# Second layer of a hybrid decoder: an earlier block transpose, other gaps in the scan, and moved turnings

## The chip, the cores and the metric

The kernel runs on one core of a Trainium2 chip. The metric is the device time of one execution in microseconds (us). The profile's engines are PE (TensorE), DVE (VectorE), ACT (ScalarE), POOL (GpSimd) and SP (SyncE), each of which takes its instructions in program order.

## The reference

Two residual layers over 512 positions of width 2048 in float32. The first is gated differential attention, which the change does not touch. The second is RWKV-7 time mixing with 32 heads of 64 channels: after one input projection and a token shift, each head keeps a 64 x 64 state S that is updated at each position, and its output is normalised, gated and projected.

```python
def step(S, inp):
    r_t, w_t, k_t, v_t, a_t, b_t = inp
    sa = jnp.einsum('bhvk,bhk->bhv', S, a_t)
    S = S * w_t[:, :, None, :] + sa[..., None] * b_t[:, :, None, :] + v_t[..., None] * k_t[:, :, None, :]
    y = jnp.einsum('bhvk,bhk->bhv', S, r_t)
    return S, y
...
kk = kk / jnp.maximum(jnp.sqrt(jnp.sum(kk * kk, axis=-1, keepdims=True)), 1e-12)
k = k * (1.0 + (a - 1.0) * k_a.astype(F32))
y = wkv7_scan(rh, heads(decay), kh, vh, -kk, kk * ah)
...
x = x + (y * silu(g)) @ w_out
```

## The kernel before

The second layer goes through 16 rounds j, each for a pair of heads (128 channels). A round is paced by projections on PE: v, then k of the next pair, the gate of an earlier pair (from j = 3, LAG), and r of the next pair. One projection is 16 slices of the 2048 inputs times three products, hH and hL being the two parts of the activations and wh and wl those of the weights: 48 matmuls pp (L129) of 128 x 512. ACT makes each wh (L115), DVE each wl (L116).

The recurrence is done in 8 chunks of 64 positions. For each pair, `gram` multiplies keys with keys and queries into gp. ACT copies parts of gp to LP and all of it to G. DVE turns LP into LT (a stream transpose, L1214), and `t_solve` solves a unit triangular system in 31 steps of two DVE instructions (tmpl, L1227, and Tm, L1230), with n the reciprocal norm. Two transposes give T (L1235) and W (L1240). `t_first` multiplies G's blocks with T into px (32 small matmuls, L1261), `t_second` finishes the blocks in TT. POOL copies W into TT (L1246) and zeroes G's upper parts (`mask_gram`, two selects for each head, L1180 and L1182).

The scan (`scan_pair`) of a pair runs one round later. For each chunk c: sm from VS and G on PE (L1353), rhs on ACT (L1356), sm from TT and rhs (L1366), VS on ACT (L1368), sm from VS and BKT (L1373), and the new state VS on DVE (L1377, or L1380 for c = 0), which the next chunk's first sm needs. `turn_keys` (L1195) and `turn_values` (L1303) turn BK and mixv by PE.

`tick` counts projection matmuls. A generator that yields n is taken up again n matmuls later: the solve by its own counts, the scan by gap, gap and gap_s (in full rounds, 3 <= j < 15, these are 7, 7 and 8). Hooks in `unit_chan` do the same at a matmul's number in a projection. `behind` ties an instruction to a matmul for the order only; the chip does not wait there. A list scheduler with priorities (scan 5000, solve 4000, urgent 2000) makes each engine's order out of this. `g.soon` and `g.later` are lists of pieces that are issued behind an ACT copy and behind a state copy of the scan.

Of the kernel before, what the change touches and what calls it, by code (L numbers as in the profile page):

```python
# [23 lines left out]
P = 128  # L24
# [928 lines left out]
C = 64  # L953
# [74 lines left out]
LAG = 3  # L1028
# [6 lines left out]
def mus(g, i, j):  # L1035
    n = i * 16 + j
    return g.mu[:, n : n + 1], g.omu[:, n : n + 1]
# [6 lines left out]
    g.nc.tensor.matmul(out, ones, l[:], start=False, stop=True)  # L1044


def soon(g):
    while g.soon:
        g.soon.pop(0)()


def stage1(g, j, k, up):
# [73 lines left out]
def gram(g, j, p):  # L1126

    nc, w, BK = g.nc, g.work, p.BK
    p.G = w.tile([P, NC_, 2, 2, C], F32, name="G1", tag="G1", bufs=2)
    halves = []  # L1130
    for c0, tag in ((0, "pb"), (4, "pc")):
        gp = [g.ps.tile([P, 512], F32, name="gp", tag=tag, bufs=2) for _ in range(2)]
        halves.append((c0, gp))
        for i in range(4):
            for h, r_ in ((0, slice(0, C)), (1, slice(C, P))):
                m = nc.tensor.matmul(gp[h][:, i * P : (i + 1) * P], BK[r_, c0 + i, :, :], p.AR[r_, c0 + i, :, :],
                                     start=True, stop=True)
    p.LP = w.tile([P, NC_, HALF], F32, name="LP", tag="tmpl", bufs=1)
    with g.tc.high_priority(offset=AHEAD):
        for c0, gp in halves:  # L1140
            for h in range(2):
                for half in range(2):
                    q, o = h * C + half * HALF, half * HALF
                    nc.scalar.copy(p.LP[q : q + HALF, c0 : c0 + 4],
                                   gp[h][q : q + HALF].rearrange("p (u x) -> p u x", u=4)[:, :, o : o + HALF])

    def grams():
        for c0, gp in halves:
            for h in range(2):
                nc.scalar.copy(p.G[:, c0 : c0 + 4, :, h, :], gp[h][:].rearrange("p (u x t) -> p u x t", u=4, x=2))  # L1150

    g.soon.append(grams)
    if not j:
        soon(g)


def norms(g, j, p, m):
# [49 lines left out]
def t_solve(g, j, p):  # L1207


    nc, w = g.nc, g.work  # L1210
    NQ = HALF // NG
    yield 9
    LT = w.tile([P, HALF, HALF], F32, name="LT", tag="LT", bufs=1)
    lt = nc.vector.transpose(LT[:].rearrange("p (r c) t -> p t r c", r=NG),  # L1214
                        p.LP[:].rearrange("p c t -> p t c")[:, :, None, :].to_broadcast([P, HALF, NG, NC_]))
    Tm = w.tile([P, NQ, HALF], F32, name="Tm", tag="Tm", bufs=1)
    tmp = w.tile([P, NQ * HALF], F32, name="tmpl", tag="tmpl", bufs=1)
    nc.gpsimd.tensor_copy(Tm[:], g.unit[:])
    n2 = p.n2
    behind(g, lt)  # L1220
    with g.tc.issue_after(lt.ins):
        nc.vector.tensor_scalar(n2[:], n2[:], 1e-24, None, ALU.max)
        nc.vector.reciprocal(n2[:], n2[:])
    for i in range(HALF - 1):
        n, s = HALF - 1 - i, i // NG + 1
        tt = tmp[:, : n * s].rearrange("p (a b) -> p a b", a=s)
        st = nc.vector.scalar_tensor_tensor(tt, LT[:, i : i + 1, i + 1 :].to_broadcast([P, s, n]), n2[:, i : i + 1],  # L1227
                                       Tm[:, 0:s, i : i + 1].to_broadcast([P, s, n]), ALU.mult, ALU.mult)
        behind(g, st)
        nc.vector.tensor_add(Tm[:, 0:s, i + 1 :], Tm[:, 0:s, i + 1 :], tt)  # L1230
        yield 3 + i % 2
    nc.vector.tensor_mul(Tm[:], Tm[:], n2[:, None, :].to_broadcast([P, NQ, HALF]))
    p.T1 = w.tile([P, NC_, HALF], F32, name="T1", tag="T1", bufs=1)
    yield 9
    tt = nc.vector.transpose(p.T1[:].rearrange("p c (q r) -> p q r c", r=NG),  # L1235
                        Tm[:].rearrange("p q (r c) -> p q r c", r=NG))
    p.W = w.tile([P, NC_, HALF], F32, name="W", tag="Tm", bufs=1)
    behind(g, tt)
    yield 4
    tt = nc.vector.transpose(p.W[:], p.T1[:])  # L1240
    behind(g, tt)
    for h in range(2):
        for half in range(2):
            o = half * HALF
            q = slice(h * C + o, h * C + o + HALF)
            nc.gpsimd.tensor_copy(g.TT[j % 2][q, :, h, o : o + HALF], p.W[q])  # L1246
# [95 lines left out]
def scan_pair(g, j, p, gap, gap_s, others):  # L1342

    nc, w, VS = g.nc, g.work, p.VS
    both = lambda ap: ap.rearrange("p h n -> p (h n)")
    p.SA = w.tile([P, NC_ - 1, C], F32, name="SA", tag="SA", bufs=1)
    for h, r_ in HEADS:
        nc.gpsimd.memset(VS[r_, 0, h, :], 0.0)  # L1350
    for c in range(NC_):
        sm = g.ps.tile([P, 512], F32, name="sm", tag="pa", bufs=1)
        nc.tensor.matmul(sm[:, 0:P], both(p.G[:, c, 0]), both(VS[:, c]), start=True, stop=True)  # L1353
        rhs = w.tile([P, C], F32, name="rhs", tag="rhs", bufs=2)
        for h, r_ in HEADS:
            rc = nc.scalar.copy(rhs[r_, :], sm[r_, h * C : h * C + C])  # L1356
        with g.tc.issue_after(rc.ins):
            soon(g)
        if c:
            for h, r_ in HEADS:  # L1360
                nc.gpsimd.tensor_copy(p.SA[r_, c - 1, :], VS[r_, c, h, :])  # L1361
        if 0 < c < NC_ - 1:
            Sg = w.tile([P, C], F32, name="Sg", tag="Sg", bufs=2)
            nc.gpsimd.tensor_scalar(Sg[:], p.SA[:, c - 1, :], p.gam[:, c : c + 1], None, ALU.mult)
        yield gap
        nc.tensor.matmul(sm[:, P : P + C], both(g.TT[j % 2][:, c]), rhs[:], start=True, stop=True)  # L1366
        for h, r_ in HEADS:
            nc.scalar.copy(VS[r_, c, h, :], sm[r_, P : P + C])  # L1368
        yield gap
        if c == NC_ - 1:  # L1370
            break
        o = P + C
        nc.tensor.matmul(sm[:, o : o + P], p.BKT[:, c, :], both(VS[:, c]), start=True, stop=True)  # L1373
        for h, r_ in HEADS:
            s_ = sm[r_, o + h * C : o + h * C + C]
            if c:
                g.state = nc.vector.scalar_tensor_tensor(VS[r_, c + 1, h, :], s_, p.gam[r_, c : c + 1], Sg[r_, :],  # L1377
                                                         ALU.mult, ALU.add)
            else:
                nc.vector.tensor_scalar(VS[r_, c + 1, h, :], s_, p.gam[r_, c : c + 1], None, ALU.mult)  # L1380
# [57 lines left out]
def layer1(g, aps):  # L1438
    nc, tc = g.nc, g.tc
    with ExitStack() as cx:  # L1440
# [5 lines left out]
        pairs = []  # L1446

        def proj(i, j, **k):
            return unit_chan(g, [(win, i * D + j * P, P)], P, **k)[0]

        def begin(j):
            c0 = j * P
            u = g.wraw.tile([RK, 2, P], F32, name="upw", tag="wraw")
            nc.sync.dma_start(out=u[:, 0, :], in_=aps["rw_decay_up"][0, :, c0 : c0 + P])
            nc.sync.dma_start(out=u[:, 1, :], in_=aps["rw_iclr_up"][0, :, c0 : c0 + P])
            up = split_act(g, u[:], w, "up")
            pairs.append(stage1(g, j, shift_mix(g, proj(1, j), P, *mus(g, 1, j), "k", 1), up))

        def receptances(j):
            def piece(f, i, p):  # L1460
# [5 lines left out]
            behind = [(39, lambda m: norms(g, j, pairs[j], m))]  # L1466
            if j:
                behind += [(6, lambda m: [mask_gram(g, pairs[j - 1], h, m) for h in range(2)]),
                           (12, piece(t_first, j - 1, pairs[j - 1])), (33, piece(t_second, j - 1, pairs[j - 1]))]
            return shift_mix(g, proj(0, j, behind=behind), P, *mus(g, 0, j), "r", 1)  # L1470

        begin(0)
# [1 line left out]
        for j in range(D // P):  # L1474
            p = pairs[j]
            if j:
# [16 lines left out]
            if j + 1 == D // P:  # L1493
                hooks.append((39, lambda m, p=p: [mask_gram(g, p, h, m) for h in range(2)]))
            stage_v(g, j, p, proj(2, j, behind=hooks))
            if j == 0:
                turn_keys(g, p, 0)
                turn_keys(g, p, 4)
                turn_values(g, p)
            if j + 1 < D // P:  # L1500
                begin(j + 1)
            if j >= LAG:
                gated(g, j - LAG, pairs[j - LAG], gate(g, j - LAG, proj(3, j - LAG)))
            if j + 1 < D // P:
                r = receptances(j + 1)
                if j:
                    with tc.high_priority(offset=AHEAD):
                        group_norm(g, j - 1, pairs[j - 1])
        chain(g, j, p, 66, 5, 6, whole=True)
        gated(g, j - 2, pairs[j - 2], gate(g, j - 2, proj(3, j - 2)))  # L1510
        gps = proj(3, j - 1)
        group_norm(g, j - 1, pairs[j - 1])
# [74 lines left out]
def body(ctx, tc, nc, aps):  # L1587
    g = Ctx()
    g.nc, g.tc = nc, tc
    g.last, g.first = None, []  # L1590
    g.chains, g.later, g.soon, g.state, g.solve = [], [], [], None, None
    g.const = ctx.enter_context(tc.tile_pool(name="const", bufs=1))
    g.hp = ctx.enter_context(tc.tile_pool(name="hp", bufs=16))
    g.wraw = ctx.enter_context(tc.tile_pool(name="wrawp", bufs=3))
# [35 lines left out]
```

## Time and profile before

| | us |
|---|---|
| median of three runs | 2161.68 (2160.67 to 2164.62) |
| the profiled execution | 2163.93 |
| its span | 2162.2 |
| PE busy | 2130.9 (99%) |
| DVE busy | 1547.3 (72%) |
| ACT busy | 1125.5 (52%) |
| POOL busy | 335.2 (16%) |

The granted TensorE clock was 0.998 of full speed. The second layer's rounds begin at about 1000 us. A full round is some 60 us long. A row of the timeline gives the start in us, the duration in us, the engine, the line, the operation and its tiles, and in brackets the idle time ahead of it and what ended it. A row of the waits gives who waited for whom, the total in us, how often, and the longest.

### The profile page before, as it was taken

To read this page: it belongs to the slowest core of one execution; us is meant where nothing else is said; L and a number is where in the kernel's file an instruction comes from. 1 tells how busy PE (TensorE), PEld (TensorE's weight loads), DVE (VectorE), ACT (ScalarE), POOL (GpSimd) and SP (SyncE) were. 2 spreads that over 40 slices of the span, in tenths; PEclk is the share of its full clock that TensorE was granted. 3 is DMA by queue.
4 is the path that set the end of the run, shared out by engine and by line. 5 is a ranking of instruction groups with operands and counts; after the bars stand their busy time and mean duration, and the time that the engine had idled before them with its cause. 6 is when DMAs were issued, how large, how long until landed. Compare 5 with 4: busy or idle time off the path is not lost.

```text
span 2162.2 us, 34954 instructions
## 1 busy us (share of the span) xinstructions
PE 2130.9 (99%) x12260; PEld 1752.8 (81%) x12260; DVE 1547.3 (72%) x4137; ACT 1125.5 (52%) x2587; POOL 335.2 (16%) x614
## 2 busy tenths in 40 slices
PE   9999999999999999999999999999999999999999
PEld 8888888888888878887777888888888888877887
DVE  5665647465656667457888988888888898887645
ACT  6443434343444455345666666666666666655333
POOL 0000000000000000011133322223333322232001
PEclk9999999999999999999999999999999999999999
DMA  6223232322223365663222233222232222345565
GB/s 196 90 86 100 79 99 87 98 89 88 97 88 97 99 198 182 185 139 87 73 69 65 67 81 85 76 77 76 78 85 77 77 68 79 89 118 186 179 169 120
DMA packets 258624, 225.77 MB, mean 104 GB/s; under 512 B 12336, under 2 KB 220480, under 8 KB 258448
## 3 DMA queue, kind: packets, MB, share of 16 engines
q1 hardware_dynamic: 239504, 188.03, 29.2%
q0 software_dynamic: 10080, 19.50, 4.5%
q10 hardware_dynamic: 8864, 16.01, 2.0%
q8 instruction: 96, 1.57, 0.3%
q14 instruction: 80, 0.66, 0.1%
HBM read 207.50 MB, written 15.99 MB: 103 GB/s over the span
## 4 chain that ended last, share of the span: by engine, by line
PE 85%; DVE 11%; issue 2%; ACT 1%; DMA 1%; POOL 0%; DVEq 0%; ACTq 0%; POOLq 0%
PE pp L129 66%; PE pt L129 5%; DVE wl L116 2%; DVE LT L1214 1%; PE sm L1353 1%; PE o L129 1%; PE sc L129 1%; PE lora L129 1%; PE sm L1373 1%; PE sm L1366 1%; DMA yr<-yd 1%; DVE tmpl L1227 1%; PE Y L1395 1%; DVE Tm L1230 1%; PE pt L346 1%
## 5 line engine op out<-in xcount | busy, mean ns | idle before, releaser
L116 DVE TENSOR_TENSOR wl<-wraw,wh 128x512 fp32r<-128x512 f32 (+1 forms) x636 | 446.9, 705 | 383.7 <-ACT wh L115 374.5
L115 ACT CAST wh<-wraw 128x512 fp32r<-128x512 f32 (+1 forms) x636 | 392.9, 619 | 516.9 <-PE pp L129 407.8
L129 PE MATMUL pp<-wh,hH 128*128 128x512 f32 x1268 | 500.3, 395 | 1.2 <-DVE prmin_rw_mu_dram L234 0.6
L129 PE MATMUL pp<-wh,hL 128*128 128x512 f32 x1268 | 497.6, 393 | 0.0
L129 PE MATMUL pp<-wl,hH 128*128 128x512 f32 x1268 | 497.1, 392 | 0.0
L129 PE MATMUL pp<-hH,wh 128*128 128x512 f32 x1024 | 417.7, 408 | 0.0
L129 PE MATMUL pp<-hH,wl 128*128 128x512 f32 x1024 | 413.3, 404 | 0.0
L129 PE MATMUL pp<-hL,wh 128*128 128x512 f32 x1024 | 413.3, 404 | 0.0
L129 PEld LDWEIGHTS pp<-wh,hH 128*128 128x128 f32 x1268 | 238.3, 188 | 50.0 <-issue 1.6
L129 PEld LDWEIGHTS pp<-wh,hL 128*128 128x128 f32 x1268 | 238.2, 188 | 48.6
L129 PEld LDWEIGHTS pp<-wl,hH 128*128 128x128 f32 x1268 | 238.4, 188 | 46.8
L129 PEld LDWEIGHTS pp<-hH,wh 128*128 128x128 f32 x1024 | 193.2, 189 | 37.8 <-issue 2.0
L129 PEld LDWEIGHTS pp<-hH,wl 128*128 128x128 f32 x1024 | 193.6, 189 | 33.4
L129 PEld LDWEIGHTS pp<-hL,wh 128*128 128x128 f32 x1024 | 193.5, 189 | 32.2
L1361 POOL COPY SA<-VS 64x64 f32<-64x64 f32 x224 | 78.0, 348 | 472.6 <-DVE VS L1377 406.9
L1227 DVE SCALAR_TENSOR_TENSOR tmpl<-LT,n,Tm 128x60 f32<-128x60 f32 (+24 forms) x496 | 136.2, 275 | 13.8
L500 POOL DMA_DIRECT2D frow<-yd x12 | 8.9, 743 | 807.6 <-DVE rs_t L67 675.8
L1230 DVE TENSOR_TENSOR Tm<-Tm,tmpl 128x60 f32<-128x60 f32 (+24 forms) x496 | 114.1, 230 | 13.2
L1356 ACT COPY rhs<-sm 64x64 f32<-64x64 f32 x256 | 52.7, 206 | 61.8 <-PE sm L1353 58.9
L1368 ACT COPY VS<-sm 64x64 f32<-64x64 f32 x256 | 53.0, 207 | 59.1 <-PE sm L1366 48.0
L1353 PEld LDWEIGHTS sm<-VS,G 128*128 128x128 f32 x256 | 45.0, 189 | 29.8 <-PE pp L129 12.9
L1377 DVE SCALAR_TENSOR_TENSOR VS<-sm,gam,Sg 64x64 f32<-64x64 f32 x192 | 54.1, 282 | 18.7 <-PE sm L1373 14.2
(339 smaller groups left out, 3261.9 us busy)
## 6 DMA issues: line engine op xcount, KB each, us to landing
wraw<-in_rw_w_in_dram SPq DMA_DIRECT2D x128, 512.0 KB, 4.0
wraw<-in_da_w_in_dram SPq DMA_DIRECT2D x254, 256.0 KB, 3.0
wraw<-in_da_w_out_dram SPq DMA_DIRECT2D x26, 512.0 KB, 4.4
wraw<-in_rw_w_out_dram SPq DMA_DIRECT2D x26, 512.0 KB, 4.1
yr<-yd SPq DMA_DIRECT2D x28, 256.0 KB, 3.4
frow<-yd POOLq DMA_DIRECT2D x12, 512.0 KB, 6.2
xq<-in_x_dram SPq DMA_DIRECT2D x16, 256.0 KB, 5.0
xd<-xq ACTq DMA_DIRECT2D x16, 256.0 KB, 3.9
```

The source lines that it names most:

```text
L115: nc.scalar.copy(hi[:], raw[:, k : k + n])
L116: nc.vector.tensor_sub(lo[:], raw[:, k : k + n], hi[:].bitcast(F32))
L129: m = nc.tensor.matmul(out, a, b, start=s, stop=e, skip_group_check=skip)
L346: nc.tensor.transpose(pt[:, c * P : (c + 1) * P], t1s[t][:, c * P : (c + 1) * P], g.ident[:])
L1214: lt = nc.vector.transpose(LT[:].rearrange("p (r c) t -> p t r c", r=NG), p.LP[:].rearrange("p c t -> p t c")[:, :, None, :].to_broadcast( ...
L1227: st = nc.vector.scalar_tensor_tensor(tt, LT[:, i : i + 1, i + 1 :].to_broadcast([P, s, n]), n2[:, i : i + 1], Tm[:, 0:s, i : i + 1].to_br ...
L1230: nc.vector.tensor_add(Tm[:, 0:s, i + 1 :], Tm[:, 0:s, i + 1 :], tt)
L1353: nc.tensor.matmul(sm[:, 0:P], both(p.G[:, c, 0]), both(VS[:, c]), start=True, stop=True)
L1356: rc = nc.scalar.copy(rhs[r_, :], sm[r_, h * C : h * C + C])
L1361: nc.gpsimd.tensor_copy(p.SA[r_, c - 1, :], VS[r_, c, h, :])
L1368: nc.scalar.copy(VS[r_, c, h, :], sm[r_, P : P + C])
L1377: g.state = nc.vector.scalar_tensor_tensor(VS[r_, c + 1, h, :], s_, p.gam[r_, c : c + 1], Sg[r_, :], ALU.mult, ALU.add)
```

## The change

Seven edits, all in the second layer. The G copies (`grams`) are split in two: the first half stays behind the rhs copies of the scan, the second half goes behind a VS copy (`g.late`). The solve's first wait goes from 9 to 5 matmuls, so that LT is asked for sooner, and a new wait of 9 (6 before j = LAG) stands between the reciprocal and the first step. In rounds 1 and 2 the steps follow each other by 2 and 3 matmuls in place of 3 and 4. `t_first` is hooked to matmul 15 of the r projection, not 12. In round 0 the turnings of keys and values move from behind the v projection into the next k projection (at 9, 15 and 27). In the last round the scan's gaps go from 4, 4 and 5 to 6, 6 and 7. The last pair's scan starts 8 matmuls into the projections that follow, not 66.

```diff
--- before.py
+++ after.py
@@ -1044,9 +1044,10 @@
     g.nc.tensor.matmul(out, ones, l[:], start=False, stop=True)
 
 
-def soon(g):
-    while g.soon:
-        g.soon.pop(0)()
+def soon(g, pieces=None):
+    pieces = g.soon if pieces is None else pieces
+    while pieces:
+        pieces.pop(0)()
 
 
 def stage1(g, j, k, up):
@@ -1144,14 +1145,15 @@
                     nc.scalar.copy(p.LP[q : q + HALF, c0 : c0 + 4],
                                    gp[h][q : q + HALF].rearrange("p (u x) -> p u x", u=4)[:, :, o : o + HALF])
 
-    def grams():
-        for c0, gp in halves:
-            for h in range(2):
-                nc.scalar.copy(p.G[:, c0 : c0 + 4, :, h, :], gp[h][:].rearrange("p (u x t) -> p u x t", u=4, x=2))
-
-    g.soon.append(grams)
+    def grams(c0, gp):
+        for h in range(2):
+            nc.scalar.copy(p.G[:, c0 : c0 + 4, :, h, :], gp[h][:].rearrange("p (u x t) -> p u x t", u=4, x=2))
+
+    g.soon.append(lambda: grams(*halves[0]))
+    g.late.append(lambda: grams(*halves[1]))
     if not j:
         soon(g)
+        soon(g, g.late)
 
 
 def norms(g, j, p, m):
@@ -1209,7 +1211,7 @@
 
     nc, w = g.nc, g.work
     NQ = HALF // NG
-    yield 9
+    yield 5
     LT = w.tile([P, HALF, HALF], F32, name="LT", tag="LT", bufs=1)
     lt = nc.vector.transpose(LT[:].rearrange("p (r c) t -> p t r c", r=NG),
                         p.LP[:].rearrange("p c t -> p t c")[:, :, None, :].to_broadcast([P, HALF, NG, NC_]))
@@ -1221,6 +1223,7 @@
     with g.tc.issue_after(lt.ins):
         nc.vector.tensor_scalar(n2[:], n2[:], 1e-24, None, ALU.max)
         nc.vector.reciprocal(n2[:], n2[:])
+    yield 9 if j >= LAG else 6
     for i in range(HALF - 1):
         n, s = HALF - 1 - i, i // NG + 1
         tt = tmp[:, : n * s].rearrange("p (a b) -> p a b", a=s)
@@ -1228,7 +1231,7 @@
                                        Tm[:, 0:s, i : i + 1].to_broadcast([P, s, n]), ALU.mult, ALU.mult)
         behind(g, st)
         nc.vector.tensor_add(Tm[:, 0:s, i + 1 :], Tm[:, 0:s, i + 1 :], tt)
-        yield 3 + i % 2
+        yield (2 if 0 < j < LAG else 3) + i % 2
     nc.vector.tensor_mul(Tm[:], Tm[:], n2[:, None, :].to_broadcast([P, NQ, HALF]))
     p.T1 = w.tile([P, NC_, HALF], F32, name="T1", tag="T1", bufs=1)
     yield 9
@@ -1365,7 +1368,9 @@
         yield gap
         nc.tensor.matmul(sm[:, P : P + C], both(g.TT[j % 2][:, c]), rhs[:], start=True, stop=True)
         for h, r_ in HEADS:
-            nc.scalar.copy(VS[r_, c, h, :], sm[r_, P : P + C])
+            vc = nc.scalar.copy(VS[r_, c, h, :], sm[r_, P : P + C])
+        with g.tc.issue_after(vc.ins):
+            soon(g, g.late)
         yield gap
         if c == NC_ - 1:
             break
@@ -1448,13 +1453,14 @@
         def proj(i, j, **k):
             return unit_chan(g, [(win, i * D + j * P, P)], P, **k)[0]
 
-        def begin(j):
+        def begin(j, turns=()):
             c0 = j * P
             u = g.wraw.tile([RK, 2, P], F32, name="upw", tag="wraw")
             nc.sync.dma_start(out=u[:, 0, :], in_=aps["rw_decay_up"][0, :, c0 : c0 + P])
             nc.sync.dma_start(out=u[:, 1, :], in_=aps["rw_iclr_up"][0, :, c0 : c0 + P])
             up = split_act(g, u[:], w, "up")
-            pairs.append(stage1(g, j, shift_mix(g, proj(1, j), P, *mus(g, 1, j), "k", 1), up))
+            pairs.append(stage1(g, j, shift_mix(g, proj(1, j, behind=turns), P, *mus(g, 1, j), "k", 1),
+                                up))
 
         def receptances(j):
             def piece(f, i, p):
@@ -1466,7 +1472,8 @@
             behind = [(39, lambda m: norms(g, j, pairs[j], m))]
             if j:
                 behind += [(6, lambda m: [mask_gram(g, pairs[j - 1], h, m) for h in range(2)]),
-                           (12, piece(t_first, j - 1, pairs[j - 1])), (33, piece(t_second, j - 1, pairs[j - 1]))]
+                           (15, piece(t_first, j - 1, pairs[j - 1])),
+                           (33, piece(t_second, j - 1, pairs[j - 1]))]
             return shift_mix(g, proj(0, j, behind=behind), P, *mus(g, 0, j), "r", 1)
 
         begin(0)
@@ -1479,7 +1486,7 @@
                 if j > 1:
                     others.append((5, lambda i=j - 2: finish_y(g, i, pairs[i])))
                 full = LAG <= j < D // P - 1
-                gaps = (7, 8) if full else (5, 6) if j == 2 else (4, 5)
+                gaps = (7, 8) if full else (5, 6) if j == 2 else (4, 5) if j == 1 else (6, 7)
                 chain(g, j - 1, pairs[j - 1], 3 if j > 1 else 22, *gaps, others)
             stage2(g, j, r, p)
 
@@ -1493,12 +1500,12 @@
             if j + 1 == D // P:
                 hooks.append((39, lambda m, p=p: [mask_gram(g, p, h, m) for h in range(2)]))
             stage_v(g, j, p, proj(2, j, behind=hooks))
+            turns = ()
             if j == 0:
-                turn_keys(g, p, 0)
-                turn_keys(g, p, 4)
-                turn_values(g, p)
+                turns = ((9, lambda m: turn_keys(g, p, 0)), (15, lambda m: turn_keys(g, p, 4)),
+                         (27, lambda m: turn_values(g, p)))
             if j + 1 < D // P:
-                begin(j + 1)
+                begin(j + 1, turns)
             if j >= LAG:
                 gated(g, j - LAG, pairs[j - LAG], gate(g, j - LAG, proj(3, j - LAG)))
             if j + 1 < D // P:
@@ -1506,7 +1513,7 @@
                 if j:
                     with tc.high_priority(offset=AHEAD):
                         group_norm(g, j - 1, pairs[j - 1])
-        chain(g, j, p, 66, 5, 6, whole=True)
+        chain(g, j, p, 8, 5, 6, whole=True)
         gated(g, j - 2, pairs[j - 2], gate(g, j - 2, proj(3, j - 2)))
         gps = proj(3, j - 1)
         group_norm(g, j - 1, pairs[j - 1])
@@ -1588,7 +1595,7 @@
     g = Ctx()
     g.nc, g.tc = nc, tc
     g.last, g.first = None, []
-    g.chains, g.later, g.soon, g.state, g.solve = [], [], [], None, None
+    g.chains, g.later, g.soon, g.late, g.state, g.solve = [], [], [], [], None, None
     g.const = ctx.enter_context(tc.tile_pool(name="const", bufs=1))
     g.hp = ctx.enter_context(tc.tile_pool(name="hp", bufs=16))
     g.wraw = ctx.enter_context(tc.tile_pool(name="wrawp", bufs=3))
```

In the order of the engines this shows at three places of a full round; round 8 (some 1480 to 1540 us) stands for all twelve. First DVE, from before LT to the state copy of chunk 1, before the change (VS is the state copy, wl the low part of a weight tile):

```order
L116 TENSOR_TENSOR wl<-wraw,wh 128x512
L1214 STREAM_TRANSPOSE LT<-LP 128x32x32
L1222 TENSOR_SCALAR n_15564<-n_15564 128x32
L1223 RECIPROCAL n_15564<-n_15564 128x32
L1227 SCALAR_TENSOR_TENSOR tmpl<-LT,n_15564,Tm 128x31
L1230 TENSOR_TENSOR Tm<-Tm,tmpl 128x31
L1227 SCALAR_TENSOR_TENSOR tmpl<-LT,n_15564,Tm 128x30
L1230 TENSOR_TENSOR Tm<-Tm,tmpl 128x30
L116 TENSOR_TENSOR wl<-wraw,wh 128x512
L1377 SCALAR_TENSOR_TENSOR VS<-sm,gam,Sg 64x64 x2
```

and after it:

```order
L1216 STREAM_TRANSPOSE LT<-LP 128x32x32
L1224 TENSOR_SCALAR n_15564<-n_15564 128x32
L116 TENSOR_TENSOR wl<-wraw,wh 128x512
L1225 RECIPROCAL n_15564<-n_15564 128x32
L1230 SCALAR_TENSOR_TENSOR tmpl<-LT,n_15564,Tm 128x31
L1233 TENSOR_TENSOR Tm<-Tm,tmpl 128x31
L1230 SCALAR_TENSOR_TENSOR tmpl<-LT,n_15564,Tm 128x30
L1233 TENSOR_TENSOR Tm<-Tm,tmpl 128x30
L1230 SCALAR_TENSOR_TENSOR tmpl<-LT,n_15564,Tm 128x29
L1233 TENSOR_TENSOR Tm<-Tm,tmpl 128x29
L116 TENSOR_TENSOR wl<-wraw,wh 128x512
L1382 SCALAR_TENSOR_TENSOR VS<-sm,gam,Sg 64x64 x2
```

The wl ahead of LT now stands behind it, and three steps instead of two stand ahead of VS.

Second PE, at the end of the scan, from the matmul that gives the state after chunk 6 to the first sm of chunk 7, before the change (pp is a projection):

```order
L1373 MATMUL sm<-VS,BKT 128x128
L129 MATMUL pp<-hH,wl 128x512
L129 MATMUL pp<-hH,wh 128x512
L129 MATMUL pp<-hL,wh 128x512
L129 MATMUL pp<-hH,wl 128x512
L129 MATMUL pp<-hH,wh 128x512
L129 MATMUL pp<-hL,wh 128x512
L129 MATMUL pp<-hH,wl 128x512
L1261 MATMUL px<-T_16073,G_15643 32x32 x16
L129 MATMUL pp<-hH,wh 128x512
L1353 MATMUL sm<-VS,G_14922 128x128
```

and after it:

```order
L129 MATMUL pp<-hH,wl 128x512
L129 MATMUL pp<-hH,wh 128x512
L129 MATMUL pp<-hL,wh 128x512
L129 MATMUL pp<-hH,wl 128x512
L129 MATMUL pp<-hH,wh 128x512
L129 MATMUL pp<-hL,wh 128x512
L129 MATMUL pp<-hH,wl 128x512
L129 MATMUL pp<-hH,wh 128x512
L1356 MATMUL sm<-VS,G_14922 128x128
L129 MATMUL pp<-hL,wh 128x512
L129 MATMUL pp<-hH,wl 128x512
L1264 MATMUL px<-T_16089,G_15643 32x32 x16
```

px now follows the sm of chunk 7; seven pp, px and one pp stood between the two sm, now eight pp.

Third POOL, beside that place, before the change (AFFINE_SELECT zeroes part of G, SA and Sg belong to the scan):

```order
L1364 TENSOR_SCALAR Sg<-SA,gam 128x64
L1180 AFFINE_SELECT G_15643<-G_15643 64x8x64
L1246 COPY TT_10024<-W 32x8x32 x4
L1361 COPY SA<-VS 64x64
L1182 AFFINE_SELECT G_15643<-G_15643 64x8x128
L1361 COPY SA<-VS 64x64
L1180 AFFINE_SELECT G_15643<-G_15643 64x8x64
L1182 AFFINE_SELECT G_15643<-G_15643 64x8x128
```

and after it:

```order
L1367 TENSOR_SCALAR Sg<-SA,gam 128x64
L1182 AFFINE_SELECT G_15643<-G_15643 64x8x64
L1184 AFFINE_SELECT G_15643<-G_15643 64x8x128
L1364 COPY SA<-VS 64x64
L1182 AFFINE_SELECT G_15643<-G_15643 64x8x64
L1364 COPY SA<-VS 64x64
L1249 COPY TT_10024<-W 32x8x32 x4
L1184 AFFINE_SELECT G_15643<-G_15643 64x8x128
```

The first large select has moved ahead of an SA copy and of the W copies into TT, right behind the first small one.

## The prediction

> **What bounds the kernel now.** I read the page's first lines, then PE's waits in the second layer, then the busy time of one round in the middle, then the timelines of DVE, PE and POOL at the places where the change puts instructions into another order. Line numbers are those of the kernel before.
>
> The page's span and engine totals (busy us, share, instructions):
>
> ```profile
> span 2162.2 us, 34954 instructions
> PE 2130.9 (99%) x12260; PEld 1752.8 (81%) x12260; DVE 1547.3 (72%) x4137; ACT 1125.5 (52%) x2587; POOL 335.2 (16%) x614
> ```
>
> PE is busy 99% of the span, so the time falls only where a wait of PE goes, and rises by every wait that is added. The view of waits for PE, from 1000 us on (engine and line, what it waited for: us in total, times, longest):
>
> ```profile
> PE sm L1353 <- DVE VS L1377: 9.3, 16, 2.2
> PE pt L1303 <- DVE Tm L1230: 3.0, 1, 3.0
> PE sm L1353 <- DVE VS L1380: 2.4, 2, 1.2
> PE px L1261 <- DVE T L1235: 1.9, 3, 0.9
> PE pt L1044 <- DVE sLx L917: 0.5, 1, 0.5
> ```
>
> These 17.1 us are all there is to gain by moving work, and nearly all of it is PE waiting for DVE. Is DVE a reserve? The window of 40 us around the solve of a full round (columns: us; PE, PEld, DVE, ACT and POOL busy with counts; clock; DMA share; GB/s):
>
> ```profile
> 1497.00:1537.00 40.00, 39.63 (x228) 32.77 (x227) 37.16 (x104) 25.23 (x61) 10.68 (x21) 1.00 0.26 69
> ```
>
> DVE is busy 37.16 of 40 us: while a solve runs it has no idle time to hide a later place in its queue. It takes instructions in program order, so what stands ahead of a state copy (VS, L1377) is paid by the next step of the scan. The twelve full rounds (j=3 to 14) run the same order, so I work out one and multiply.
>
> **The change part by part.** *The state after chunk 1, twelve times.* DVE and then PE before (start, duration):
>
> ```profile
> 1497.52 2.23 DVE L1214 STREAM_TRANSPOSE LT<-LP 128x1024 f32<-128x1024 f32 x1
> 1500.28 0.25 DVE L1227 SCALAR_TENSOR_TENSOR tmpl<-LT,n,Tm 128x31 f32<-128x31 f32 x1
> 1500.79 0.25 DVE L1227 SCALAR_TENSOR_TENSOR tmpl<-LT,n,Tm 128x30 f32<-128x30 f32 x1
> 1501.19 0.69 DVE L116 TENSOR_TENSOR wl<-wraw,wh 128x512 fp32r<-128x512 f32 x1
> 1501.91 0.60 DVE L1377 SCALAR_TENSOR_TENSOR VS<-sm,gam,Sg 64x64 f32<-64x64 f32 x2
> ...
> 1499.64 0.38 PE L1373 MATMUL sm<-VS,BKT 128*128 128x128 f32 x2
> 1501.67 0.39 PE L129 MATMUL pp<-hH,wh 128*128 128x512 f32 x1
> 1501.89 0.39 PE L129 MATMUL pp<-hL,wh 128*128 128x512 f32 x1
> 1502.65 0.46 PE L1353 MATMUL sm<-VS,G 128*128 128x128 f32 x2 [0.37 <-DVE VS L1377]
> ```
>
> The matmul that gives the state ends at 1500.02, yet the copy starts at 1501.91: it stands in DVE's queue behind two solve steps and a wl, and PE waits 0.37. In the new order LT starts one wl sooner, but the wl then stands behind it, and three steps instead of two come ahead of the copy. The same work plus one step: a step costs 0.51 (1500.28 to 1500.79). This wait is the end of the path already, so I add 0.51; bounds 0.46 (the two instructions without a gap, 0.25 and the 0.21 of a Tm, below) and 0.6 (should POOL slow one of them a little).
>
> *The state after chunk 6, twelve times.* DVE, PE and POOL there, with two rows of round 1 (1117 us) for comparison:
>
> ```profile
> 1529.44 0.21 DVE L1230 TENSOR_TENSOR Tm<-Tm,tmpl 128x16 f32<-128x16 f32 x1
> 1530.17 0.63 DVE L1227 SCALAR_TENSOR_TENSOR tmpl<-LT,n,Tm 128x8 f32<-128x8 f32 x1
> 1533.60 0.42 DVE L1240 STREAM_TRANSPOSE W<-T 128x256 f32<-128x256 f32 x1
> 1533.94 0.71 DVE L949 SCALAR_TENSOR_TENSOR mixv<-pp,prmin_rw_mu_dram,mixv 128x511 f32<-128x511 f32 x1
> 1534.57 0.58 DVE L1377 SCALAR_TENSOR_TENSOR VS<-sm,gam,Sg 64x64 f32<-64x64 f32 x2
> 1537.82 1.11 DVE L1108 TENSOR_TENSOR gam<-m 128x7 f32<-128x7 f32 x1
> 1117.38 1.09 DVE L1230 TENSOR_TENSOR Tm<-Tm,tmpl 128x54 f32<-128x54 f32 x1
> ...
> 1532.58 0.38 PE L1373 MATMUL sm<-VS,BKT 128*128 128x128 f32 x2
> 1534.19 0.40 PE L129 MATMUL pp<-hH,wl 128*128 128x512 f32 x1
> 1534.51 0.69 PE L1261 MATMUL px<-T,G 32*32 32x32 f32 x32
> 1535.14 0.50 PE L129 MATMUL pp<-hH,wh 128*128 128x512 f32 x1
> 1535.48 0.38 PE L1353 MATMUL sm<-VS,G 128*128 128x128 f32 x2
> ...
> 1529.71 1.07 POOL L1180 TENSOR_SCALAR_AFFINE_SELECT G<-G 64x512 f32<-64x512 f32 x1
> 1537.31 1.61 POOL L1182 TENSOR_SCALAR_AFFINE_SELECT G<-G 64x1024 f32<-64x1024 f32 x1
> 1117.25 1.16 POOL L1182 TENSOR_SCALAR_AFFINE_SELECT G<-G 64x1024 f32<-64x1024 f32 x1
> ```
>
> Three things come together. First, PE: between the two sm stand seven projection matmuls, the 32 small px, and one more projection matmul. t_first's hook goes from 12 to 15, and in the new order px comes after this sm. The gap is then eight plain matmuls, which start 0.22 apart (1501.67 to 1501.89). The seventh starts at 1534.19, so the new sm is due two starts later, at 1534.63, 0.85 sooner than 1535.48. The copy ends at 1535.15 and an sm starts 0.14 after its copy (1502.51 to 1502.65), so 1535.29 is the soonest and the slack is 0.19. Cover lost: 0.85 - 0.19 = 0.66. Second, DVE: ahead of this copy the new order has one more step (+0.51) and no longer W (1533.60 to 1533.94, -0.34): +0.17. Third, POOL: the large select L1182, until now behind the W copies, directly follows the L1180 that started at 1529.71, as nothing it needs lies between. It then runs from 1530.78 on, among the instructions ahead of the copy. What that does shows in round 1, where the two selects already run one behind the other: the Tm that meets L1182 takes 1.09, where a Tm takes 0.21 alone (1529.44), and ends at 1118.47, with the select (1118.41). The tmpl at 1530.17 ends with L1180 too (1530.80 and 1530.78), and gam at 1537.82 with L1182 (1538.93 and 1538.92). I charge 1.09 - 0.21 = 0.88, the nearest row. It is bounded by 0 (the select meets a DVE instruction that does not mind it) and by its whole 1.16.
>
> [...]
>
> Sum at this place: 0.66 + 0.17 + 0.88 = 1.71; bounds 0.66 (the cover alone) and 0.66 + 0.3 + 1.16 = 2.1, where 0.3 is the step with most of W still ahead. Both places: 12 x (0.51 + 1.71) = +26.6 us.
>
> *What costs nothing in full rounds.* The second half of the G copies (grams) goes behind an ACT copy of the scan; ACT is busy 25.23 of 40 us, and the selects that need G come a whole projection later. If that cover went, two of the four copies would fall ahead of a VS of the scan, half of this row, 1.03:
>
> ```profile
> 1556.73 2.06 ACT L1150 COPY G<-gp 128x512 f32<-128x512 f32 x4
> ```
>
> The later W delays only its POOL copies into TT, which the next chain wants several microseconds later. LT's earlier place takes a wl 2.2 us later; PE was never seen to wait for one in these rounds.
>
> *The first round.* Rows of PE and DVE:
>
> ```profile
> 1057.55 0.63 PE L1303 MATMUL pt<-ident,mixv 128*128 128x128 f32 x4 [3.01 <-DVE Tm L1230]
> ...
> 1059.89 0.69 DVE L116 TENSOR_TENSOR wl<-wraw,wh 128x512 fp32r<-128x512 f32 x1 [0.61 <-ACT wh L115]
> 1067.80 0.69 DVE L116 TENSOR_TENSOR wl<-wraw,wh 128x512 fp32r<-128x512 f32 x1 [0.74 <-ACT wh L115]
> 1082.95 0.69 PE L1261 MATMUL px<-T,G 32*32 32x32 f32 x32 [0.38 <-DVE T L1235]
> ```
>
> The turnings move into the next projection, so the 3.01 goes. But at 1082.95 px waits for T, the end of the same solve, and DVE worked at it all the time but for 0.61 + 0.74: what PE gains sooner it mostly gives back at px. I take these 1.35 as -1.4; bounds -0.6 and -3.2.
>
> *Rounds 1 and 2.* Faster steps (2 + i%2) end the solves sooner. px's waits there (1.9 - 0.38 = 1.5) and the first states' 2.4 could go: -3.9 at best. But the chunk-0 state stands behind one more step (+0.5 a round), and the norms wait (sLx, 0.5 once) can come twice. I take half of the waits, -1.9, and +1.4: -0.5; bounds -4 and +2.
>
> *The last round.*
>
> ```profile
> 1929.98 0.72 PE L1353 MATMUL sm<-VS,G 128*128 128x128 f32 x2 [2.20 <-DVE VS L1377]
> ```
>
> Gaps of 6 and 7 give DVE two matmuls more at each step: the 2.20 goes. Each later state has less hidden, some 0.2 left. The final chain starts 58 matmuls sooner, while projections still cover it. -2.0; bounds -4 and +1.
>
> Sum: 26.6 - 1.4 - 0.5 - 2.0 = +22.7. The profiled execution took 2163.93 (span 2162.2, the rest around it), the median of the three runs is 2161.68, 2.25 lower; on the median 2161.68 + 22.7 = 2184.4 us.
>
> **The rivals.** *The select blocks nothing.* If it falls beside transposes or copies from PSUM, its 0.88 drops out: 12 x (0.51 + 0.83) - 3.9 = +12.2, 2173.9 us. For it: DVE was busy 37.16 of 40 us beside POOL's 10.68, so most of its instructions do run beside POOL. Against: the three ends that fall together.
>
> *The chunk-6 state has slack that I do not see*, as DVE may arrive with less backlog: only 12 x 0.51 - 3.9 = +2.2 stays, 2163.9 us, no change to measure. Against: 37.16 of 40.
>
> *Faster.* LT ahead of the wl ends sooner, and the scan's copy gets ahead of the solve: the chunk-1 wait goes (12 x 0.37 = 4.4) and nothing new appears: -4.4 - 3.9 = -8.3, 2153.4 us. It decides if the copy starts by 1501.54 (1501.91 - 0.37). Against it stands the order itself: three steps precede it.
>
> **How the numbers follow.** 0.60 for the forecast, 0.23 for the first rival, 0.08 for no change, 0.09 for faster. A measurement here tells about 0.2%, 4.3 us, from nothing. Faster rival: 0.09 and 0.01 from the edge of the no-change case; same 0.06; slower 0.84. The range leaves out the last two rivals (0.17). Its low end is the first rival with the early and last rounds at their best (-11.2 instead of -3.9), 7.3 less: 2166.6; its high end is 12 x (0.6 + 2.1) = 32.4 with them at their worst (-0.6 + 2 + 1): +34.8, 2196.5.
>
> **What would show it.** In the waits, sm <- VS should stand some 24 to 28 times in place of 16: about 0.9 at chunk 2 of each full round and 1.2 to 1.7 at chunk 7, while pt <- Tm and px <- T go. gam should be short in full rounds, with another DVE instruction of 1 us or more beside POOL's L1182. A chunk-7 wait under 1.0 without such an instruction makes the first rival right; no chunk-7 wait, the second; a chunk-2 wait under 0.37, the third.

## The result, and the profile after

The changed kernel took 2192.7 us (median of four runs, 2191.32 to 2193.17). The kernel before, run beside it, took 2161.18 (2160.56 to 2164.62). The ratio is 1.0142, with a 95% interval from 1.0124 to 1.0159: 31.5 us slower. The profiled execution took 2193.17. The lines of its page and of PE's waits from 1000 us on that answer to those shown before:

```profile
span 2191.2 us, 34905 instructions
PE 2138.0 (98%) x12260; PEld 1755.5 (80%) x12260; DVE 1550.3 (71%) x4137; ACT 1129.6 (52%) x2587; POOL 338.8 (15%) x614
...
PE sm L1356 <- DVE VS L1382: 29.6, 28, 1.5
PE pt L1044 <- DVE sLx L917: 3.2, 2, 1.9
PE sm L1356 <- DVE VS L1385: 2.9, 2, 1.7
PE px L1264 <- DVE T L1238: 2.5, 3, 1.9
PE sm L1369 <- ACT rhs L1359: 0.9, 2, 0.7
```

The wait of sm for the state VS went from 9.3 us in 16 places to 29.6 in 28: twelve new places, one for each full round. PE also became busier by 7.1 us with the same 12260 matmuls, which waits alone cannot explain.

In a full round the two places are these (PE's timeline, round 8; the bracket is PE's wait):

```profile
1515.97 0.46 PE L1356 MATMUL sm<-VS,G 128*128 128x128 f32 x2 [0.76 <-DVE VS L1382]
1549.67 0.46 PE L1356 MATMUL sm<-VS,G 128*128 128x128 f32 x2 [1.53 <-DVE VS L1382]
```

The first is chunk 2, the second chunk 7. From chunk 2 of round 3 to chunk 2 of round 14 passed 659.12 us before (1203.05 to 1862.17) and 688.77 after (1202.61 to 1891.38): 29.65 more in eleven rounds. Seven of these last about 62.05, 2.13 over the old 59.92, and four last about 63.6, 1.57 more again. The windows view shows what the four have: half clock, that is a stretch in which TensorE's granted clock is half. Round 3, PE's row at chunk 7, then stretches of 4 us behind it (columns as before; the clock stands ahead of the last two):

```profile
1236.29 0.46 PE L1356 MATMUL sm<-VS,G 128*128 128x128 f32 x2 [1.51 <-DVE VS L1382]
...
1236.00:1240.00 4.00, 3.71 (x44) 2.94 (x44) 3.97 (x6) 3.73 (x9) 3.79 (x6) 0.79 0.07 19
1240.00:1244.00 4.00, 4.00 (x60) 3.15 (x63) 2.06 (x5) 2.13 (x7) 2.12 (x4) 0.78 0.17 66
1244.00:1248.00 4.00, 4.00 (x69) 2.99 (x58) 1.62 (x6) 1.35 (x3) 0.55 (x2) 1.00 1.00 256
...
1238.78 0.63 PE L129 MATMUL pp<-hH,wh 128*128 128x512 f32 x1
1239.20 0.63 PE L129 MATMUL pp<-hL,wh 128*128 128x512 f32 x1
```

The granted clock falls to 0.79 and 0.78 in these stretches; single stretches of 1 us show 0.50, and neighbouring projection matmuls start 0.42 apart (1238.78, 1239.20) in place of 0.23. For some 3.4 us PE runs at half speed, which costs some 1.6 us and counts as busy time.

What each part of the layer gained or lost shows in the first matmul of the v projection of rounds 0, 1, 3 and 15, first before, then after the change:

```profile
1038.10 0.39 PE L129 MATMUL pp<-hH,wh 128*128 128x512 f32 x1
1080.59 0.40 PE L129 MATMUL pp<-hH,wh 128*128 128x512 f32 x1
1187.69 0.39 PE L129 MATMUL pp<-hH,wh 128*128 128x512 f32 x1
1907.06 0.39 PE L129 MATMUL pp<-hH,wh 128*128 128x512 f32 x1
...
1035.99 0.39 PE L129 MATMUL pp<-hH,wh 128*128 128x512 f32 x1
1076.75 0.39 PE L129 MATMUL pp<-hH,wh 128*128 128x512 f32 x1
1186.88 0.39 PE L129 MATMUL pp<-hH,wh 128*128 128x512 f32 x1
1937.72 0.39 PE L129 MATMUL pp<-hH,wh 128*128 128x512 f32 x1
```

Round 0 took 42.49 us and now takes 40.76 (-1.73). Rounds 1 and 2 took 107.10 and now 110.13 (+3.03). The twelve full rounds took 719.37 and now 750.84 (+31.47): in round numbers 12 x 2.13 = 25.6 at the two places and 4 x 1.57 = 6.3 of half clock. From round 15 to the end it is some -1.7. Together that is +31.1, near the 31.5 between the medians. The two spans differ by 29.0 only, because the profiled execution of the kernel before came to round 0 2.11 us later than the other, ahead of the rounds that the change reorders.

### The profile page after: what moved, and what is told of

Same layout as the page of the kernel before. It is cut to its first block, busy times and chain, and to the rows that moved or that the text cites. A ratio compares the mean times of both kernels' runs of the same rounds, so it can differ in the third digit from the quotient of the medians.

```text
span 2191.2 us, 34905 instructions
## 1 busy us (share of the span) xinstructions
PE 2138.0 (98%) x12260; PEld 1755.5 (80%) x12260; DVE 1550.3 (71%) x4137; ACT 1129.6 (52%) x2587; POOL 338.8 (15%) x614
## 3 DMA queue, kind: packets, MB, share of 16 engines
q8 instruction: 96, 1.57, 0.3%
## 4 chain that ended last, share of the span: by engine, by line
PE 86%; DVE 10%; issue 2%; ACT 1%; DMA 1%; POOL 0%; ACTq 0%; DVEq 0%; POOLq 0%
PE pp L129 66%; PE pt L129 5%; DVE tmpl L1230 1%; PE sm L1356 1%; DVE wl L116 1%; PE gp L1137 1%; PE o L129 1%; PE sc L129 1%; PE lora L129 1%; DVE Tm L1233 1%; PE sm L1378 1%; PE sm L1369 1%; DVE VS L1382 1%; DMA yr<-yd 1%; PE Y L1400 1%
## 5 line engine op out<-in xcount | busy, mean ns | idle before, releaser
L1230 DVE SCALAR_TENSOR_TENSOR tmpl<-LT,n,Tm 128x60 f32<-128x60 f32 (+24 forms) x496 | 149.1, 301 | 13.7
L1364 POOL COPY SA<-VS 64x64 f32<-64x64 f32 x224 | 72.9, 326 | 536.1 <-DVE VS L1382 474.5
L1356 PE MATMUL sm<-VS,G 128*128 128x128 f32 x256 | 51.9, 285 | 32.6 <-DVE VS L1382 29.6
```

## Experiments

The times of each run stand beside runs of the kernel before on the same chip (2161.2 to 2163.1 in these comparisons), and ratios are to those. Line numbers shift by a few from one kernel to another.

### One part undone

**e1, px ahead of sm again.**

```diff
-                           (15, piece(t_first, j - 1, pairs[j - 1])),
+                           (12, piece(t_first, j - 1, pairs[j - 1])),
```

> The changed kernel with t_first's hook back at 12; DVE's and POOL's orders in full rounds stay those of the changed kernel, only px goes ahead of the sm of chunk 7 again. Cover theory (mine): the wait at chunk 7 falls from 1.5 by px's 0.85 to some 0.65 in each of twelve rounds, 10.2 us, and the four stretches of half TensorE clock that follow waits of 1.5 (1.57 us each, 6.3) go with it: 2192.7 - 16.5 = 2176.2 us. If the half clock does not come from these waits: 2182.5. If px has no cover to give, the wait being DVE's alone whatever stands before sm: 2192.7.

Measured: 2176.91 us, ratio 1.0063 (1.0048 to 1.0078). The number is the one expected; the way to it is not, so the match is luck. The wait at chunk 7 is gone wholly, and PE waits for T ahead of px instead (waits of PE):

```profile
PE sm L1356 <- DVE VS L1382: 11.5, 16, 1.3
PE px L1264 <- DVE T L1238: 11.2, 16, 2.0
```

With the new DVE order T ends so late that px cannot stand ahead without waiting. So px's place is worth 16 us in all, half clock included, but the old place does not bring back the old cover. No half clock is left in the full rounds.

**e2, the solve's waits of full rounds undone; e5, these and the G copies.**

```diff
# e2
-    yield 5
+    yield 9 if LAG <= j < 15 else 5
...
-    yield 9 if j >= LAG else 6
+    if j < LAG:
+        yield 6
+    elif j == 15:
+        yield 9
# e5, besides
-    g.soon.append(lambda: grams(*halves[0]))
-    g.late.append(lambda: grams(*halves[1]))
+    g.soon.append(lambda: [grams(*x) for x in halves])
```

> The changed kernel with the solve's waits of full rounds back at 9 and none: DVE's order and POOL's there are nearly those of before, px stays behind the sm of chunk 7. Cover theory: chunk 2 waits 0.37 again (-0.38 x 12 = -4.6), chunk 7 keeps only the lost cover, about 0.65 of 1.66 (-12.1), no half clock (-6.3): about 2169.7 us. If DVE has slack that hides px's cover: 2162. If the solve's place hardly matters and px's order is all: 2188 (only chunk 2 moves).

> The changed kernel with the solve's waits of full rounds and the G copies in one piece as before; in full rounds only px's place (behind the sm of chunk 7) is left of the change. Cover theory: chunk 2 waits 0.37 again, chunk 7 waits 0.5 to 0.65 for the cover that px gave, no half clock: 12 x 0.6 = 7.2 over the kernel with the old full rounds (2160.7): 2168 us. It also tells what puts the third step ahead of the chunk-1 state: if the G copies in two pieces do, as the wait of 0.88 at chunk 2 with the old solve suggests, the wait is 0.37 here; if px's place does, it stays 0.88 and the time 2175.8.

Measured: e2 2175.77 us, ratio 1.0057 (1.0042 to 1.0072); e5 2171.29, ratio 1.0040 (1.0025 to 1.0055). Chunk 2 and chunk 7 of round 8, first e2, then e5:

```profile
1508.90 0.46 PE L1359 MATMUL sm<-VS,G 128*128 128x128 f32 x2 [0.86 <-DVE VS L1385]
1541.59 0.46 PE L1359 MATMUL sm<-VS,G 128*128 128x128 f32 x2 [0.52 <-DVE VS L1385]
...
1506.87 0.46 PE L1358 MATMUL sm<-VS,G 128*128 128x128 f32 x2 [0.39 <-DVE VS L1384]
1539.55 0.46 PE L1358 MATMUL sm<-VS,G 128*128 128x128 f32 x2 [0.52 <-DVE VS L1384]
```

In e5 only px's place is left of the change in a full round: it costs a wait of 0.52 at chunk 7, and a round lasts 60.70, 0.78 more than 59.92. e2 missed its expected 2169.7 because chunk 2 did not go back to 0.37: it waits 0.86 to 0.91, one solve step more. e5 against e2 shows what puts that step ahead of the state: the G copies in two pieces. They take nothing on DVE themselves; DVE's order, which the scheduler makes, has a third step ahead of the state in e2 and two in e5, with ACT's copies in other places. Why the scheduler does so is not shown.

**e6, the G copies alone undone** (the last edit of e5 by itself).

> The changed kernel with the G copies in one piece as before; on DVE the second half of the third step goes behind the chunk-1 state, all else in full rounds stays. Queue theory: the wait at chunk 2 falls from 0.75 by a Tm's 0.2 to 0.25, about 0.5, and chunk 7 stays at 1.5 with its few half clocks: 2192.7 - 12 x 0.23 = 2190 us. Rival, that the copies on ACT are what delays the state: chunk 2 back at 0.37 and 2188 us. Rival, that ACT's copies hide nothing and cost nothing: 2192.7.

Measured: 2187.77 us, ratio 1.0117 (1.0100 to 1.0134). Chunk 2 waits 0.52 to 0.55 and chunk 7 still 1.51 to 1.53, as the queue theory had it: the third step's tmpl still stands ahead of the state, its Tm behind it. Two full rounds had half clock here.

**e3, the large selects later on POOL.**

```diff
-                (6, lambda m: [mask_gram(g, pairs[j - 1], h, m) for h in range(2)]),
+                (6, lambda m: [mask_gram(g, pairs[j - 1], h, m, 1) for h in range(2)]),
+                (21, lambda m: [mask_gram(g, pairs[j - 1], h, m, 2) for h in range(2)]),
```

Part 1 of mask_gram is the small select, part 2 the large one.

> The changed kernel with the large selects hooked to matmul 21 of the r projection, so that on POOL they stand behind the small ones, the SA and the TT copies; PE's and DVE's orders are untouched. Block theory (mine): the 0.88 that the select takes from DVE ahead of the chunk-6 state goes: chunk 7 waits about 0.65, no half clock: 2192.7 - 10.6 - 6.3 = 2175.8 us. Rival, that the select blocks nothing: 2192.7 and a wait of 1.5 as before. If it is the small selects that block: 2192.7 too, with a long DVE instruction still there.

Measured: 2181.56 us, ratio 1.0083 (1.0068 to 1.0098); chunk 7 waits 1.00 to 1.04, and no half clock is left. The fall of 0.49 is less than 0.88. POOL and DVE ahead of the chunk-6 state, first in the changed kernel, then in e3:

```profile
1543.49 1.69 POOL L1184 TENSOR_SCALAR_AFFINE_SELECT G<-G 64x1024 f32<-64x1024 f32 x1
1544.08 1.12 DVE L1230 SCALAR_TENSOR_TENSOR tmpl<-LT,n,Tm 128x16 f32<-128x16 f32 x1
...
1537.46 2.37 POOL L1183 TENSOR_SCALAR_AFFINE_SELECT G<-G 64x512 f32<-64x512 f32 x2
1539.23 0.62 DVE L1232 SCALAR_TENSOR_TENSOR tmpl<-LT,n,Tm 128x16 f32<-128x16 f32 x1
```

In the changed kernel the tmpl ends at 1545.20, with the large select (1545.18), and takes 0.90 more than the 0.22 of a tmpl alone. In e3 the second small select moved up into the free place and the same tmpl ends with it (1539.85 and 1539.83), 0.40 more than alone. 0.90 - 0.40 = 0.50 is what the wait lost. The large select's price was as forecast; the experiment did not leave the place empty.

**e4, all of it undone in rounds 3 to 14** (the edits of e2 and e5, and px at 12 from pair 3 on).

> The changed kernel with rounds 3 to 14 in the order of the kernel before (solve's waits, px, G copies), so that only the edits of rounds 0 to 2 and 15 and of the last chain remain. By the trace the twelve rounds cost 12 x 2.13 + 6.3 = 31.9 and the rest gave 2.7: 2158.5 us, 2.7 under the kernel before. By my prediction's terms, 3.9 under it: 2157.3. Rival, that the ends of the layer cost time too: at or above 2161.2.

Measured: 2160.69 us against 2162.69, ratio 0.9990 (0.9980 to 0.9999). **e12, the last round's edits alone** (of the change only the last round's solve waits, its gaps, its late G copies and the last chain's delay of 8):

> The kernel before with the edits of the last round and the last chain alone; rounds 0 to 14 in the old order. Before, PE waited 2.20 there and half clock followed (1.6); with the edits 1.3 and 0.7 are waited and no half clock follows. By my prediction's term: -2.0. By the traces of e4, from chunk 2 of round 14 to the end: -1.4 us, the rest of e4's -2.0 coming from rounds 0 to 2. Rival: the early rounds gave all of it and this is 0.

Measured: 2160.73 us against 2162.52, ratio 0.9993 (0.9984 to 1.0002). The edges are worth 2.0 us, and the last round by itself 1.8, an effect that its interval does not quite part from none. Rounds 0 to 2 together so gave about nothing, as far as two intervals of some 2 us each way can tell. In e4's trace v of rounds 0, 1 and 3 starts at 1036.30, 1077.06 and 1186.07: round 0 is 1.73 shorter than before, rounds 1 and 2 are 1.91 longer. PE's waits in e4:

```profile
PE sm L1362 <- DVE VS L1388: 7.1, 16, 1.3
PE pt L1044 <- DVE sLx L917: 3.0, 2, 1.9
PE sm L1362 <- DVE VS L1391: 2.9, 2, 1.7
PE px L1270 <- DVE T L1244: 2.4, 3, 1.9
```

The 3.0 of the turnings is gone, and sLx has grown from 0.5 to 3.0, px from 1.9 to 2.4 and VS of chunk 0 from 2.4 to 2.9.

### The half clock

**e7, a longer wait at the same place.**

```diff
+        if c == NC_ - 2 and gap_s == 8:
+            junk = g.small.tile([P, 1], F32, name="junk", tag="junk", bufs=1)
+            for _ in range(2):
+                nc.vector.reduce_sum(junk[:], sm[:, o : o + P], AX.X)
```

The sm of chunk 7 is held ahead of the projection matmul that is issued next.

> The changed kernel with two small reductions of the sm tile on DVE ahead of the state after chunk 6 (their result is not used) in rounds 3 to 14, between which W falls, and the sm of chunk 7 held to its place among the projections (one matmul later). The wait at chunk 7 should be some 2.1 instead of 1.5, 7 us in all. Clock theory: a wait of PE of 1.5 brings half clock in a third of the cases and a longer one in more: at least 7 of the 12 rounds, 1.6 us each, so 2192.7 + 7 + 5 or more: 2205 us. Rival, that half clock comes at times of its own, whatever the wait: 4 rounds, 2200 us.

Measured: 2215.14 us, ratio 1.0243 (1.0222 to 1.0263). The trace puts the wait on the matmul behind sm:

```profile
PE pp L129 <- DVE VS L1392: 31.0, 12, 2.8
...
1429.00:1433.00 4.00, 3.16 (x40) 2.50 (x41) 3.94 (x8) 2.76 (x8) 3.54 (x6) 0.79 0.07 17
```

The waits are 2.54 to 2.77, longer than meant, and ten of twelve are followed by half clock, against four of twelve at 1.5. The rival (times of its own, whatever the wait) falls.

### Can the waits be taken away?

**e8, a wider gap after chunk 1**, on e4:

```diff
-        yield gap_s
+        yield gap_s + (2 if c == 1 and gap_s == 8 else 0)
```

> The kernel with the old full rounds (2160.7) and a gap after chunk 1 of 10 matmuls instead of 8 in rounds 3 to 14; the norms' two matmuls also come ahead of that sm, so it has about 0.9 more cover than the 0.37 wait needs. Queue theory: the wait at chunk 2 goes (start to start 0.54), no other state is later than its new place: 2160.7 - 12 x 0.54 = 2154.2 us. Rival: the later states each stand behind another solve step and a wait of the same length comes at chunk 3 or 7: 2160.

Measured: 2171.52 us, ratio 1.0040 (1.0025 to 1.0055): the rival, and worse. Chunk 2 waits no more, but the state after chunk 2 now stands behind another step and a wl, and chunk 3 waits 0.91 to 0.93 in eleven full rounds and 1.24 in the last.

**e9, the steps put behind the chunk-1 state**, on e4 (with three of the four selects and px moved too):

```diff
+    else:
+        yield 13
...
-        yield (2 if 0 < j < LAG else 3) + i % 2
+        yield (2 if 0 < j < LAG or LAG <= j < 15 and i < 6 else 3) + i % 2
...
-        yield gap_s
+        yield gap_s + (1 if c == 1 and gap_s == 8 else 0)
...
+                (24, lambda m: mask_gram(g, pairs[j - 1], 1, m, 1)),
+                (24, lambda m: [mask_gram(g, pairs[j - 1], h, m, 2) for h in range(2)]),
+                (15 if j <= LAG else 18, piece(t_first, j - 1, pairs[j - 1])),
```

> The kernel of e4 (2160.7) with, in rounds 3 to 14: the first solve step 13 matmuls after LT, so that the chunk-1 state stands ahead of all steps; the first six steps a matmul closer to each other; one matmul more after chunk 1; px four matmuls behind the sm of chunk 7; the second small select and both large ones behind W's copies on POOL. Queue theory: the state after chunk 1 is ready 0.9 sooner in DVE's queue, none of the later ones comes later than its sm (closest: chunk 3 with 0.12 and chunk 7 with 0.09 to spare, by counting the instructions ahead of each), so the 0.54 of each round goes: 2160.7 - 6.5 = 2154.2 us. Rival: the steps put off come back as a wait at a later chunk, as in e8: 2160 or more.

Measured: 2163.97 us, ratio 1.0004 (0.9995 to 1.0014). The wait at chunk 2 is gone and one of 0.50 to 0.53 stands at chunk 7, where 0.09 had been counted to spare: px no longer covers that place, and the wait is that of e5. **e10** moves two hooks of the early rounds besides:

```diff
-            behind = [(39, lambda m: norms(g, j, pairs[j], m))]
+            behind = [(45 if 0 < j < LAG else 39, lambda m: norms(g, j, pairs[j], m))]
...
-                (15 if j <= LAG else 18, piece(t_first, j - 1, pairs[j - 1])),
+                (24 if j == LAG else 15 if j < LAG else 18, piece(t_first, j - 1, pairs[j - 1])),
```

> e9 with two more hooks moved in the early rounds: the norms of pairs 1 and 2 from matmul 39 to 45 of the r projection (PE waited 1.9 and 1.3 for their sLx) and px of pair 2 from 15 to 24 (PE waited 1.9 for T). If these waits are only a matter of place, some 3 to 4 us go: 2151 us. Rival: n comes later by the same six matmuls, the solves of rounds 1 and 2 start later and T is waited for instead: 2154 to 2156.

Measured: 2160.37 us, ratio 0.9988 (0.9979 to 0.9997), 3.6 under e9: the expected gain, from e9's time. **e11** gives the chunk-7 state three matmuls more:

```diff
-        yield gap_s + (1 if c == 1 and gap_s == 8 else 0)
+        yield gap_s + ((0, 1, 0, 0, 0, 0, 3)[c] if gap_s == 8 else 0)
...
-                (24 if j == LAG else 15 if j < LAG else 18, piece(t_first, j - 1, pairs[j - 1])),
+                (24 if j == LAG else 15 if j < LAG else 21, piece(t_first, j - 1, pairs[j - 1])),
```

> e10 (2160.4) with three matmuls more between the state after chunk 6 and its sm in rounds 3 to 14, and px held four matmuls behind that sm. Queue theory: the wait of 0.52 at chunk 7, the only one left in a full round, is covered by 3 x 0.23 = 0.69 and goes: 12 x 0.52 to 0.6 = 6 to 7 us: 2154 us, under both kernels. Rival: the chain ends three matmuls later and what follows it (T's second half, the next group norm) is waited for: 2160.

Measured: 2151.39 us against 2162.52, ratio 0.9950 (0.9936 to 0.9964). Of PE's waits for VS, six places are left, none in a full round:

```profile
PE sm L1366 <- DVE VS L1392: 2.8, 4, 1.3
PE sm L1366 <- DVE VS L1395: 2.6, 2, 1.7
PE pt L1044 <- DVE sLx L917: 2.0, 2, 1.2
```

It beats both kernels, the one before by 11 us. From chunk 2 of round 7 to chunk 2 of round 8 pass 59.39 us, in e10 60.15. That is 0.76 less for a wait of 0.51: such a wait cost PE more than its row, as in e5.

## Why the prediction was right

Forecast 2184.4 us and slower, in a range from 2166.6 to 2196.5; measured 2192.7. The direction and the two places were right; the size, +22.7 against +31.5, was short. The full rounds gave 31.5 where 26.6 was forecast, because of half clock, which no step held, and rounds 1 and 2 gave +3.0 where -0.5 was forecast. That 2192.7 still lies under the range's high end is in part luck: the range holds no half clock, and its high end rests on 2.1 at chunk 6, which did not come.

*The state after chunk 1, 0.51 forecast.* The wait grew by 0.38 (0.37 to 0.75). The step's price was right: e2 against e5 gives 0.86 - 0.39 = 0.47. LT's earlier place gives some 0.1 back (0.86 in e2, 0.76 in the changed kernel), where the prediction had it change nothing. The third step was in the sum, read off DVE's order. What failed is the part on edits that cost nothing: it put the split of the G copies there, looking only at ACT's spare time. With the old solve the split alone moves the whole step ahead of the state (e2 against e5). With the new solve the step's tmpl is ahead without it (0.53 in e6, 0.37 before), and the split adds its Tm (0.53 to 0.75).

*The state after chunk 6, 1.71 forecast.* The wait is 1.49 to 1.53, and sm starts 1.88 to 1.92 after the matmul ahead of it, some 1.67 more than the 0.23 of plain matmuls. Cover lost: 0.66 forecast, a wait of 0.52 and 0.78 of round time in e5. Select: 0.88 forecast, 0.90 on the trace. One step more and W less, 0.17, was not tried by itself; 1.53 less 0.52 and 0.90 leaves 0.11 for it. The rival that the select blocks nothing fell with the 1.12 of that tmpl and with e3. Its condition holds on the trace before, where a transpose and an instruction that reads PSUM took little or no longer beside the selects (LT 2.28 in round 0, 2.18 to 2.24 in the others; mixk<-pp 0.74 at 1170.56, 0.75 alone); but a tmpl stands there now. gam, which no longer meets the large select, went from 1.11 to 0.35 in the full rounds.

*The first round, -1.4.* It was -1.73. The size was right, the place was not: the prediction let px give back what PE gained, but px kept its wait (0.38, now 0.39), and the wait for sLx went from 0.48 to 1.91.

*Rounds 1 and 2, -0.5.* They were +3.03, and +1.91 in e4: the sign was wrong. The prediction took half of the waits to go. The waits for the state after chunk 0, 1.16 and 1.19, became 1.67 and 1.19, sLx now waits 1.33 in round 1, and in round 2 px waits for T, with half clock behind it (PE, then the windows view):

```profile
1173.32 1.00 PE L1264 MATMUL px<-T,G 32*32 32x32 f32 x32 [1.90 <-DVE T L1238]
...
1174.00:1175.00 1.00, 1.00 (x14) 0.84 (x10) 0.97 (x3) 0.63 (x2) 0.94 (x2) 0.50 0.00 0
```

The prediction named the chunk-0 state (0.5 a round) and sLx (0.5, twice) as risks, not px.

*The last round, -2.0.* -1.8 in e12. The prediction counted the wait of 2.20 at 1929.98 and some 0.2 for each later state. It left out the half clock behind that wait (a stretch of 1 us of the windows view of the kernel before), which went too, while a wait of 1.3 stands in its place:

```profile
1931.00:1932.00 1.00, 1.00 (x5) 0.81 (x4) 0.86 (x5) 0.93 (x2) 0.00 (x0) 0.50 1.02 306
```

*What no step held:* half clock, behind the 1.90 above and behind waits of 1.5, where it cost 6.3 us in the full rounds. Forecast waits of 0.9 and 1.2 to 1.7 were priced at their own length only. With 4 x 1.57 the forecast would have been 2190.7.

The signs: 28 waits of sm for VS, within the 24 to 28 named; chunk 2 at 0.75 where about 0.9 was named; chunk 7 at 1.5 within 1.2 to 1.7; a DVE instruction of 1.12 beside the large select. pt's wait for Tm went, but px's for T did not (2.5).

## What to carry to other kernels

Where one engine is busy 99% and waits for another whose queue is full, read the order ahead of each instruction on the path, and price an edit by what it moves there, even an edit on a third engine (the G copies on ACT: 0.47 at chunk 2, e2 against e5). Instructions that only fill time between two ends of a dependence, as px did, are cover: moving px cost a wait of 0.52 and 0.78 of round time (e5), where its length less the slack, 0.66, was forecast. A wait taken away in a paced chain shifts every later deadline, so the later slacks must be counted again before the gain is booked (0.91 to 0.93 came at chunk 3 in e8, 0.50 to 0.53 at chunk 7 in e9).

## What the runs showed of the hardware

Half clock followed some of PE's waits, and in the full rounds of the changed kernel it cost 1.57 us each time besides the wait. In all fourteen traces here, none of 57 waits between 1.0 and 1.42 us in the second layer was followed by half clock, 6 of 25 near 1.5 were (four of the changed kernel's twelve at chunk 7, two of e6's), 8 of 18 near 1.9 to 2.0 (the changed kernel's 1.90 for T, not its 1.91 for sLx), and 11 of 15 above 2.1 (the 2.20 of the kernel before and ten of e7's twelve, not the 3.01 of the kernel before and of e12); none of 14 between 1.6 and 1.85. In the traces before and after the change the half clock lasts 3.41 us behind each of these waits, of 1.49 to 2.20.

Equal waits differ by where they fall. In the changed kernel half clock begins at 1173.46, 1238.32, 1426.05, 1613.78 and 1862.96, as the clock of short windows gives it; the second reaches to some 1241.72 by these two (1241.73 by the 0.85 of the stretch from 1241.70 to 1241.80):

```profile
1238.00:1239.00 1.00, 1.00 (x4) 0.80 (x4) 1.00 (x3) 0.95 (x4) 0.96 (x2) 0.66 0.00 0
1241.00:1242.00 1.00, 1.00 (x5) 0.77 (x4) 0.00 (x0) 0.42 (x1) 1.00 (x1) 0.64 0.70 262
```

These starts are 64.86, 187.73, 187.73 and 249.18 apart, which is 19, 55, 55 and 73 times 3.413: all five lie on marks 3.413 us apart. In the kernel before half clock begins at 984.55 and 1930.04, 945.49 apart, 277 times 3.4133. Of the changed kernel's twelve waits at chunk 7, the four that half clock followed had 1.31, 1.35, 1.39 and 1.51 us behind the last mark, and half clock began at the next one; the eight others had 0.08 to 1.27. That alone does not decide, for a wait of 1.67 in round 1 (1089.86 to 1091.53) that lay wholly between two marks (1088.13 and 1091.54) brought none. What decides besides was not shown.
